# One accumulated row per token: the scatter of the experts' rows in a hybrid decoder layer

## The chip, the cores and the metric

One Trainium2 chip, of which the kernel uses 1 core. The metric is the device time of one execution in microseconds. The kernel before was run three times: 1439.99, 1440.33 and 1444.06 us, median 1440.33 us. All tensors of the interface are float32.

## What is computed

One layer over 1024 tokens of 1024 numbers: a norm with conditioning, a mixer of two branches (a convolution and an mLSTM), a residual, a second norm, a mixture of experts, a residual and a final norm. The change concerns the mixture of experts. Cut to what matters:

```
p_grp = softmax(h @ w_rg + b_rg);  g_sel = argmax(p_grp)             # one of 4 groups per token
le_sel = (h @ w_re + b_re)[token, g_sel]                              # 8 experts of that group
top_p, top_e = top_k(softmax(le_sel), 2)                              # two experts per token
w_tok = p_g * top_p / sum(top_p)
ys = (silu(xb @ w_e_gate[e]) * (xb @ w_e_up[e])) @ w_e_down[e]        # per expert, on its tokens' rows
y[token] = sum over its two experts of w_tok * ys
x = x + gate2 * y;   out = rmsnorm(x, g_final)
```

Every token thus gets two rows of 1024 numbers, from two different experts of the same group.

## The kernel before

**Order of the work.** Everything is issued in one hand-written order. The mixer comes first. Its projection is a list of jobs of 48 matrix products each (`z_cols`, L473); after the first half of a job and after its end `fill` (L290) takes one step from each of a few queues of small work: `lat` and `lat2` (the mLSTM, the convolution's norm) and `aux` (first the conditioning's remaining columns, then `clear_y`). When the jobs are over, `drain` (L299) runs what the queues still hold, and then the branches' own projections begin (`branch`, L1004; their results are named `yTrue`). At its end the mLSTM generator waits until `aux` is empty (L879), then releases buffers and gives out eight more steps (L894 to L904): each transposes one tile of 128 tokens on TensorE (`psT`, four 128x128 transposes), scales it on ScalarE (`hs`) and splits it on VectorE (`bHt`, `bLt`).

**The buffer for experts' rows.** `y_d` is a DRAM buffer of 2T = 2048 rows of 4 KB: row t for a token's first expert, row T+t for its second. `clear_y` (L448) fills it with zeros, 16 stores of 512 KB through SP's queue, with two steps of `aux` for each.

**The experts.** Their rows are worked in 25 blocks of 128 rows, in 24 units (L1460). The 16 fullest experts have a large block each (0 to 15; block 24 is a second block of expert 2's place); the other 16 share the 8 small blocks 16 to 23, two experts to a block, 64 rows each. One large and one small block alternate as large, large, small. For each block, `st_slots` (L1681) finds by a product on TensorE which token stands in which of the 128 rows (`idx`, and the row's weight `wsl`), and GpSimd gathers these tokens' rows from DRAM (`gather`, L1602, into one of three buffers `xg`). `st_x` transposes them (`tpx`), `st_gu` multiplies with the gate and up weights, `st_act` and `st_h` make the hidden rows, `st_down` (L1731) multiplies with the down weights and scales the result into `ye`. The weights come through SP's queue in pieces of 1 MB into six buffers `big`; for a large block ScalarE and VectorE split each piece into a high and a low part (`wh`, `wl`) and TensorE makes three products, for a small block the pieces go into TensorE as they are. `scatter` (L1607) then writes the rows of `ye` to `y_d`: one indirect DMA from GpSimd's queue; rows of the block that hold no token have an index out of bounds and are left out. The column of `idx` that it uses, the second, is the row of `y_d`; the first column is the token. Each such DMA waits for the one before it on `y_d`.

**The end.** The last two blocks (14 and 15, `LATE`) are not scattered: their rows stay in SBUF as `lates` and are put in token order by products with a selection matrix (`selT`, results `yl`). When the last unit begins, `load_y` (L1811) issues 16 loads of 512 KB from `y_d` through SP's queue, for eight tiles of 128 tokens two rows each. `sum_y` (L1826) adds them up: for tiles 0 and 1 straight into the residual `mg` (tile 0 on GpSimd, tile 1 on VectorE, two additions each), for the others on GpSimd into the first of the two. The final loop (L1900) makes, for each tile, the products `yl`, for tiles 4 to 7 also a product of the summed rows with the identity into the same PSUM; VectorE adds the PSUM to `mg` (and for tiles 2 and 3 the summed rows as well), ScalarE sums the squares, GpSimd makes the factor `r`, VectorE scales (`final_out`, L1894), and the tile is stored.

Of the kernel before, what the change touches and what calls it, by code (L numbers as in the profile page):

```python
# [18 lines left out]
P = 128  # L19
# [23 lines left out]
def hybrid_layer_kernel(ctx: ExitStack, tc: tile.TileContext, x, c, w_ada, b_ada, g_norm1, w_in, b_if,  # L43
# [11 lines left out]
    def tt(o, a, b, op, eng=V):  # L55
        return eng.tensor_tensor(out=o, in0=a, in1=b, op=op)  # L56

    def ts(o, a, s1, op0, s2=None, op1=None, eng=V):
        if op1 is None:
            return eng.tensor_scalar(out=o, in0=a, scalar1=s1, scalar2=None, op0=op0)  # L60
        return eng.tensor_scalar(out=o, in0=a, scalar1=s1, scalar2=s2, op0=op0, op1=op1)
# [4 lines left out]
    def mm(o, l, r, start, stop):  # L66
        return PE.matmul(o, l, r, start=start, stop=stop)  # L67
# [7 lines left out]
    mod_d = dram.tile([32, P], F32, name="mod_d")  # L75
    nM_d = dram.tile([32, P], F32, name="nM_d")
    h2_d = dram.tile([T, D], F32, name="h2_d")
    y_d = dram.tile([2 * T, D], F32, name="y_d")


    cst = ctx.enter_context(tc.tile_pool(name="cst", bufs=1, side="left"))
# [366 lines left out]
    def clear_y():  # L448
        zero = ml.tile([P, 256], F32, name="zero")
        G.memset(zero, 0.0)  # L450
        for i in range(2 * NT):
            nc.sync.dma_start(y_d[i * P:(i + 1) * P, :].rearrange("p (a n) -> p a n", n=256),
                              zero.unsqueeze(1).broadcast_to([P, 4, 256]))
            yield 0
            yield 0
# [1148 lines left out]
                             in_offset=bass.IndirectOffsetOnAxis(ap=idx[:, 0:1], axis=0),  # L1604
                             bounds_check=T - 1, oob_is_err=False)

    def scatter(src, idx):  # L1607
        G.indirect_dma_start(out=y_d[:, :], out_offset=bass.IndirectOffsetOnAxis(ap=idx[:, 1:2], axis=0),  # L1608
                             in_=src, in_offset=None, bounds_check=2 * T - 1, oob_is_err=False)

    def ovf_slots(pool, bv, name):

# [118 lines left out]
    def st_down(unit):  # L1731
        py = {b: [mps.tile([P, 512], F32, tag="m", name=f"py{b}_{hf}") for hf in range(2)] for b in unit}
        for k in range(4):
            if unit[0] in SMALL:
                if k % 2 == 0:
                    wab = [W.take() for _ in range(4)]
                for hf in range(2):
                    for n, h_ in enumerate(HALVES):
                        mm(py[unit[0]][hf][h_, :], R[unit[0]]["g"][:, k, h_],
                           wab[2 * n + k % 2][:, hf * 512:(hf + 1) * 512], k == 0, k == 3)  # L1740
                if k % 2:
                    W.used()
                continue
            wh, wl = W.take()
            for b in unit:
                gH, gL = R[b]["g"]
                for i, (a, b_) in enumerate(((gH, wh), (gL, wh), (gH, wl))):
                    for hf in range(2):
                        mm(py[b][hf], a[:, k, :], b_[:, hf * 512:(hf + 1) * 512], k == 0 and i == 0, k == 3 and i == 2)
        for b in unit:  # L1750
            d = R.pop(b)
            y = wp.tile([P, WB], F32, tag="raw", bufs=2, name=f"ye{b}")[:, 0:D]
            late = b in blocks[-LATE:]
            yhl = [wp.tile([P, WB], F32R, tag="whl", bufs=6, name=f"y{x_}{b}")[:, 0:D] for x_ in "hl"] if late else None
            for hf in range(2):
                sl = slice(hf * 512, (hf + 1) * 512)
                stt(y[:, sl], py[b][hf], d["wsl"], gt2[:, sl], OP.mult, OP.mult)
                if b == blocks[-1]:
                    split(yhl[0][:, sl], yhl[1][:, sl], y[:, sl])
            if late:  # L1760
                lates.append(yhl + [y])
            else:
                scatter(y, d["idx"])


    for r in range(FIX):
# [41 lines left out]
    def into_x1(t, a, eng=V):  # L1808
        tt(x1_of(t), x1_of(t), k3(a), OP.add, eng=eng)

    def load_y():  # L1811

        n = W.bigs_loaded
        bufs = [W.big[(n + i // 2) % len(W.big)][:, i % 2 * D:(i % 2 + 1) * D] for i in range(9)]
        bufs += [xgs[(len(blocks) + i) % 3] for i in range(3)]
        a = uo.tile([P, 2, D], F32, tag="ar", bufs=2, name="yra")
        bufs += [a[:, 0, :], a[:, 1, :]]
        bufs += [cvp.tile([P, D], F32, tag="s", bufs=4, name="yrs"), mo.tile([P, D], F32, tag="tHL", bufs=2, name="yrt")]
        gf[0] = cvp.tile([P, D], F32, tag="s", bufs=4, name="gfr")
        on_all_rows(gf[0], vec[:, 120:128])  # L1820
        for t in range(NT):
            for i in range(2):
                yin[t, i] = bufs[2 * t + i]
                nc.sync.dma_start(yin[t, i], y_d[i * T + t * P:i * T + (t + 1) * P, :])

    def sum_y(t):  # L1826
        if t < 2:
            for i in range(2):
                into_x1(t, yin[t, i], V if t else G)
        else:  # L1830
            tt(yin[t, 0], yin[t, 0], yin[t, 1], OP.add, eng=G)


    W.limit = len(W.pieces) - 2
# [52 lines left out]
    def final_norm(t, pool, o):  # L1887
        r3_ = pool.tile([P, 1], F32, tag="r3", bufs=4, name=f"r3_{t}")
        S.activation(k3(o), x1_of(t), AF.Square, scale=float(D) ** -0.5, accum_out=r3_)
        ts(r3_, r3_, RMS_EPS, OP.add, eng=G)  # L1890
        rsqrt(r3_, r3_, 1)
        return r3_

    def final_out(t, o, r3_):  # L1894
        stt(k3(o), x1_of(t), r3_, k3(gf[0]), OP.mult, OP.mult)
        (S if t == NT - 1 else nc.sync).dma_start(out[t * P:(t + 1) * P, :], o)
# [3 lines left out]
    for t in range(NT + 1):  # L1900
        if t < NT:
            if t % 2:
                ps = [mps.tile([P, 512], F32, tag="m", name=f"yl{t}_{hf}") for hf in range(2)]
            else:
                ps_ = zps.tile([P, 2, 512], F32, tag="z", name=f"yl{t}")
                ps = [ps_[:, hf, :] for hf in range(2)]
            on_pe = t >= NT - 4
            for n in range(LATE):
                for i in range(2):
                    for hf in range(2):  # L1910
                        mm(ps[hf], selT[:, n, t * P:(t + 1) * P], lates[n][i][:, hf * 512:(hf + 1) * 512],
                           n == 0 and i == 0, not on_pe and n == LATE - 1 and i == 1)
            if on_pe:
                for hf in range(2):
                    mm(ps[hf], ident, yin[t, 0][:, hf * 512:(hf + 1) * 512], False, True)
            if t + 4 < NT:
                sum_y(t + 4)
            if t % 2:
                for hf in range(2):
                    o_ = x1_of(t)[:, hf * 4:hf * 4 + 4, :]  # L1920
                    tt(o_, o_, k3(ps[hf]), OP.add)
            else:
                into_x1(t, ps_.rearrange("p a b -> p (a b)"))
            if 2 <= t and not on_pe:
                into_x1(t, yin[t, 0])
            r3[t] = final_norm(t, mo, yin[t, 1])
        if t > 0:
            final_out(t - 1, yin[t - 1, 1], r3[t - 1])

    order.__exit__(None, None, None)  # L1930

# [104 lines left out]
```

## Time and profile before

| what | value |
|---|---|
| three runs | 1439.99, 1440.33, 1444.06 us |
| the profiled execution | 1436.36 us, its span 1434.6 us |
| TensorE busy | 1304.0 us, 91% of the span |
| VectorE, ScalarE, GpSimd busy | 70%, 36%, 24% |
| mean granted clock of TensorE | 0.958 of full speed |
| DMA | 336.60 MB, mean 235 GB/s |

The profile cuts the span into 40 slices of 35.9 us and gives the busy share of each engine in each. Its rows are the place to see stages: the mixer until about 790 us, the routing until about 860 us, the experts until about 1395 us, the end.

### The profile page before, as it was taken

Reading aid. Unit: us, or ns where it says so; the run is one execution under the profiler, and the core shown is the slowest. Engines: PE = TensorE matmul, PEld = TensorE weight load, DVE = VectorE, ACT = ScalarE, POOL = GpSimd, SP = SyncE. Lnnn points to the kernel's source line nnn. Section 1 sums busy time; section 2 is a strip of 40 time slices with the busy share of each in tenths; the row PEclk is TensorE's granted clock in tenths of the full one; section 3 lists DMA queues with packets and bytes.
Section 4 is the critical chain, followed back from the end, with each engine's and each line's share of the span. In section 5 each row is a group of like instructions: output and inputs, shape, how many; then the busy total and the mean of one; then the engine's idle time right before and its main releaser. Section 6 shows DMA issues by size and latency. Waiting matters only on the chain. (4 is left out here: it accounts for less than half of the span.)

```text
span 1434.6 us, 17769 instructions
## 1 busy us (share of the span) xinstructions
PE 1304.0 (91%) x6659; PEld 981.1 (68%) x6659; DVE 1008.0 (70%) x1375; ACT 522.4 (36%) x692; POOL 337.6 (24%) x270
## 2 busy tenths in 40 slices
PE   4799888999999999999999669999999999999976
PEld 3687888879878888778888545656465655655554
DVE  6979998889966661654557786357676766764587
ACT  5233143333622225311232533225354453533442
POOL 3333455231231310124223211001011111111033
PEclk9799999999999999999999779999999999999998
DMA  9433443333454343454522449799999999999982
GB/s 287 127 118 133 140 140 118 132 118 89 132 179 131 124 135 123 162 166 159 182 70 78 187 167 377 308 379 418 413 415 396 412 399 405 414 382 415 405 332 118
DMA packets 121017, 336.60 MB, mean 235 GB/s; under 512 B 12465, under 2 KB 74205, under 8 KB 96096
## 3 DMA queue, kind: packets, MB, share of 16 engines
q1 hardware_dynamic: 106208, 291.34, 54.1%
q0 software_dynamic: 14528, 43.56, 8.1%
q8 instruction: 53, 0.87, 0.2%
q10 hardware_dynamic: 192, 0.54, 0.1%
q14 instruction: 36, 0.29, 0.1%
HBM read 302.85 MB, written 41.45 MB: 240 GB/s over the span
## 5 line engine op out<-in xcount | busy, mean ns | idle before, releaser
L56 DVE TENSOR_TENSOR wl<-big,wh 128x1024 fp32r<-128x1024 f32 x192 | 233.7, 1254 | 101.4 <-ACT wh L148 100.1
L148 ACT CAST wh<-big 128x1024 fp32r<-128x1024 f32 x192 | 193.6, 1048 | 181.6 <-DMA big<-in_w_e_gate_dram 94.4
L64 DVE SCALAR_TENSOR_TENSOR cacc<-u,vec,cacc 128x1024 f32<-128x1024 f32 x120 | 211.2, 1760 | 2.9
L67 PE MATMUL gu<-wh,tHLx 128*128 128x512 f32 x544 | 174.6, 402 | 2.8 <-ACT wh L148 1.4
L67 PE MATMUL z<-hH,wh 128*128 128x512 f32 x512 | 167.4, 409 | 7.4 <-DVE hH L377 5.1
L67 PE MATMUL z<-hL,wh 128*128 128x512 f32 x512 | 164.5, 403 | 1.2 <-DVE hL L56 1.2
L67 PE MATMUL z<-hH,wl 128*128 128x512 f32 x512 | 163.3, 400 | 0.0
L67 PE MATMUL gu<-big,tFx 128*64 128x512 f32 x512 | 122.3, 621 | 0.0
L67 PEld LDWEIGHTS gu<-wh,tHLx 128*128 128x128 f32 x544 | 99.9, 189 | 30.6 <-ACT wh L148 7.6
L67 PEld LDWEIGHTS z<-hH,wh 128*128 128x128 f32 x512 | 97.0, 193 | 29.7 <-ACT hH L380 5.1
L67 PE MATMUL gu<-wl,tHLx 128*128 128x512 f32 x272 | 109.3, 402 | 8.7 <-DVE wl L56 8.6
L67 PEld LDWEIGHTS z<-hL,wh 128*128 128x128 f32 x512 | 98.3, 192 | 25.7 <-DVE hL L56 1.9
L67 PEld LDWEIGHTS z<-hH,wl 128*128 128x128 f32 x512 | 98.1, 192 | 23.8
L1608 POOL DMA_INDIRECT y_d<-ye,idx x23 | 33.2, 1445 | 330.2 <-DVE ye L64 326.6
L56 DVE TENSOR_TENSOR wl<-raw,wh 128x1024 fp32r<-128x1024 f32 (+1 forms) x45 | 70.6, 1573 | 39.7 <-ACT wh L148 39.7
L56 POOL TENSOR_TENSOR acc<-acc,ar 128x1024 f32<-128x1024 f32 x24 | 70.8, 2951 | 62.3 <-ACT ar L572 53.4
L67 PEld LDWEIGHTS gu<-big,tFx 128*64 128x64 f32 x512 | 36.3, 142 | 69.6 <-issue 67.3
L67 PE MATMUL py<-wh,tHLh 128*128 128x512 f32 x272 | 78.4, 411 | 0.1
L67 PE MATMUL zt<-wh,hH 128*128 128x256 f32 (+1 forms) x256 | 74.9, 292 | 2.6 <-DVE u L56 1.3
L67 PE MATMUL zt<-wl,hH 128*128 128x256 f32 (+1 forms) x256 | 73.7, 288 | 2.8 <-DVE wl L56 2.8
L67 PE MATMUL zt<-wh,hL 128*128 128x256 f32 (+1 forms) x256 | 74.1, 290 | 0.0
L67 PE MATMUL o<-woH,mHL 128*128 128x512 f32 x256 | 72.8, 400 | 0.0
(404 smaller groups left out, 2209.3 us busy)
## 6 DMA issues: line engine op xcount, KB each, us to landing
big<-in_w_e_gate_dram SPq DMA_DIRECT2D x64, 1024.0 KB, 9.2
big<-in_w_e_up_dram SPq DMA_DIRECT2D x64, 1024.0 KB, 6.0
big<-in_w_e_down_dram SPq DMA_DIRECT2D x64, 1024.0 KB, 9.3
raw<-in_w_in_dram SPq DMA_DIRECT2D x38, 512.0 KB, 4.4
ar<-in_w_ada_dram SPq DMA_DIRECT2D x16, 1024.0 KB, 6.3
araw<-in_w_ada_dram SPq DMA_DIRECT2D x8, 1024.0 KB, 10.2
y_d<-zero SPq DMA_DIRECT2D x16, 512.0 KB, 5.2
big<-y_d SPq DMA_DIRECT2D x9, 512.0 KB, 9.7
```

Of the source, the lines that this page charges most:

```text
L56: return eng.tensor_tensor(out=o, in0=a, in1=b, op=op)
L64: return V.scalar_tensor_tensor(out=o, in0=a, scalar=s, in1=b, op0=op0, op1=op1)
L67: return PE.matmul(o, l, r, start=start, stop=stop)
L148: S.copy(h, src)
L1608: G.indirect_dma_start(out=y_d[:, :], out_offset=bass.IndirectOffsetOnAxis(ap=idx[:, 1:2], axis=0), in_=src, in_offset=None, bounds_check= ...
```

## The change

`y_d` has one row per token. `clear_y` clears 8 tiles in place of 16. The scatter uses the first column of `idx` (the token) and adds to the row in DRAM (`compute_op`) in place of writing it. In a small block the same token may stand twice, once in each half; such a block is therefore sent in two DMAs, each with the other half's indices pushed out of bounds by two small VectorE operations. `load_y` loads 8 tiles. `sum_y` adds tiles 0 to 3 to `mg` (even ones on GpSimd, odd ones on VectorE) and has nothing to do for the others.

```diff
-    y_d = dram.tile([2 * T, D], F32, name="y_d")
+    y_d = dram.tile([T, D], F32, name="y_d")
...
-        for i in range(2 * NT):
+        for i in range(NT):
             nc.sync.dma_start(y_d[i * P:(i + 1) * P, :].rearrange("p (a n) -> p a n", n=256),
...
-    def scatter(src, idx):
-        G.indirect_dma_start(out=y_d[:, :], out_offset=bass.IndirectOffsetOnAxis(ap=idx[:, 1:2], axis=0),
-                             in_=src, in_offset=None, bounds_check=2 * T - 1, oob_is_err=False)
+    past = rp.tile([P, 2], F32, name="past")
+    for n in range(2):
+        ts(past[:, n:n + 1], pio, 64.5, (OP.is_gt, OP.is_lt)[n], float(2 * T), OP.mult)
+
+    def scatter(b, src, idx):
+
+        rows_ = [idx[:, 0:1]]
+        if b in SMALL:
+            rows_ = []
+            for n in range(2):
+                rows_.append(mo.tile([P, 1], I32, tag=f"half{n}", bufs=2, name=f"half{n}_{b}"))
+                tt(rows_[n], idx[:, 0:1], past[:, n:n + 1], OP.add)
+        for r_ in rows_:
+            G.indirect_dma_start(out=y_d[:, :], out_offset=bass.IndirectOffsetOnAxis(ap=r_, axis=0),
+                                 in_=src, in_offset=None, bounds_check=T - 1, oob_is_err=False, compute_op=OP.add)
...
-                scatter(y, d["idx"])
+                scatter(b, y, d["idx"])
...
         for t in range(NT):
-            for i in range(2):
-                yin[t, i] = bufs[2 * t + i]
-                nc.sync.dma_start(yin[t, i], y_d[i * T + t * P:i * T + (t + 1) * P, :])
+            yin[t] = bufs[t]
+            nc.sync.dma_start(yin[t], y_d[t * P:(t + 1) * P, :])
 
     def sum_y(t):
-        if t < 2:
-            for i in range(2):
-                into_x1(t, yin[t, i], V if t else G)
-        else:
-            tt(yin[t, 0], yin[t, 0], yin[t, 1], OP.add, eng=G)
+        if t < NT - 4:
+            into_x1(t, yin[t], V if t % 2 else G)
...
-            if t + 4 < NT:
-                sum_y(t + 4)
...
-            if 2 <= t and not on_pe:
-                into_x1(t, yin[t, 0])
```

Three places show what this moves.

**TensorE, between the last job of the mixer's projection (`z5000`) and the branches' projection (`yTrue`).** Before, the seven transposed tiles psT1 to psT7 stand there in a row:

```order
L67 MATMUL z5000_4226<-hH_110,wl39_4090 128x512 x2
L897 MATMUL psT1_4293<-ident_118,WT0_2483 128x128 x4
L897 MATMUL psT2_4308<-ident_118,WT0_2483 128x128 x4
L897 MATMUL psT3_4323<-ident_118,WT0_2483 128x128 x4
L897 MATMUL psT4_4335<-ident_118,WT1_2540 128x128 x4
L897 MATMUL psT5_4347<-ident_118,WT1_2540 128x128 x4
L897 MATMUL psT6_4359<-ident_118,WT1_2540 128x128 x4
L897 MATMUL psT7_4371<-ident_118,WT1_2540 128x128 x4
L67 MATMUL yTrue_0_4408<-uH0_4217,wh40_4150 128x512 x2
```

Now three of them do:

```order
L67 MATMUL z5000_4269<-hH_110,wl39_4098 128x512 x2
L897 MATMUL psT5_4336<-ident_118,WT1_2540 128x128 x4
L897 MATMUL psT6_4351<-ident_118,WT1_2540 128x128 x4
L897 MATMUL psT7_4363<-ident_118,WT1_2540 128x128 x4
L67 MATMUL yTrue_0_4400<-uH0_4090,wh40_4181 128x512 x2
```

`aux` is empty earlier, since the clearing takes 16 steps in place of 32; psT0 to psT4 have moved up, one by one between the products of the last three jobs.

**GpSimd, around a small block (18) among the experts.** Before, each scatter is followed by a gather for a later block (`xg`):

```order
L1608 DMA y_d_92<-ye4_7608,idx4_6936 2048x1024
L1603 DMA xg2_5929<-h2_d_91,idx19_7669 128x1024
L1608 DMA y_d_92<-ye18_7774,idx18_7135 2048x1024
L1603 DMA xg0_5927<-h2_d_91,idx7_7853 128x1024
L1608 DMA y_d_92<-ye5_7979,idx5_7319 2048x1024
```

Now the small block's rows go in two DMAs, and the gather for block 7 stands behind both:

```order
L1620 DMA y_d_92<-ye4_7617,idx4_6938 1024x1024
L1603 DMA xg2_5921<-h2_d_91,idx19_7678 128x1024
L1620 DMA y_d_92<-ye18_7783,half0_18_7786 1024x1024
L1620 DMA y_d_92<-ye18_7783,half1_18_7788 1024x1024
L1603 DMA xg0_5919<-h2_d_91,idx7_7869 128x1024
L1620 DMA y_d_92<-ye5_7995,idx5_7328 1024x1024
```

The second half waits until the first has landed, and the gather waits its turn behind it.

**VectorE, in the final loop.** Before (tiles 1 to 3):

```order
L56 TENSOR_TENSOR mg_4387<-mg_4387,yl2_10563 128x8x128
L56 TENSOR_TENSOR mg_4387<-mg_4387,big0_4954 128x8x128
L64 SCALAR_TENSOR_TENSOR big1_4955<-mg_4387,r3_1_10557,gfr_10404 128x1024
L56 TENSOR_TENSOR mg_4387<-mg_4387,yl3_0_10581 128x4x128
L56 TENSOR_TENSOR mg_4387<-mg_4387,yl3_1_10582 128x4x128
L56 TENSOR_TENSOR mg_4387<-mg_4387,big2_5885 128x8x128
L64 SCALAR_TENSOR_TENSOR big0_4954<-mg_4387,r3_2_10575,gfr_10404 128x1024
```

Now:

```order
L56 TENSOR_TENSOR mg_4379<-mg_4379,yl2_10599 128x8x128
L64 SCALAR_TENSOR_TENSOR xg2_5921<-mg_4379,r3_1_10593,gfr_10452 128x1024
L56 TENSOR_TENSOR mg_4379<-mg_4379,yl3_0_10615 128x4x128
L56 TENSOR_TENSOR mg_4379<-mg_4379,yl3_1_10616 128x4x128
L64 SCALAR_TENSOR_TENSOR xg0_5919<-mg_4379,r3_2_10609,gfr_10452 128x1024
```

The additions of the summed rows for tiles 2 and 3 are gone from the loop (they stand ahead of it, one of them on GpSimd), and so are GpSimd's four additions inside the loop.

## Rows read from the trace of the kernel before

**Rows 1.** The second part of the profile's page: by 40 slices of 35.9 us the busy tenths of TensorE and of the DMA engines.
```profile
PE   4799888999999999999999669999999999999976
...
DMA  9433443333454343454522449799999999999982
```

**Rows 2.** The table of stretches: start and end, length, busy us of PE, PEld, DVE, ACT and POOL (instructions), granted TensorE clock, DMA share, GB/s.
```profile
580.00:585.00 5.00, 2.35 (x11) 1.98 (x11) 4.93 (x8) 5.00 (x18) 0.00 (x0) 0.80 0.19 79
...
860.00:1366.00 506.00, 479.90 (x2414) 291.79 (x2413) 314.92 (x357) 210.31 (x254) 56.96 (x43) 0.98 0.98 396
900.00:950.00 50.00, 49.90 (x245) 30.60 (x246) 23.71 (x27) 15.12 (x19) 4.21 (x4) 1.00 0.81 315
1040.00:1080.00 40.00, 36.89 (x192) 24.61 (x194) 30.20 (x35) 18.02 (x22) 4.99 (x4) 0.97 1.01 413
1080.00:1088.00 8.00, 8.00 (x49) 2.82 (x45) 2.82 (x3) 3.53 (x5) 0.98 (x1) 0.91 0.89 345
```

**Rows 3.** The DMA view of the experts' stretch, 860 to 1366 us: the queue of GpSimd (packets, MB, packet time as a share of 16 engines over the stretch), then GpSimd's issues with their number and the median us to landing.
```profile
q0 software_dynamic: 6192, 14.72, 7.6%
...
y_d<-ye,idx POOLq DMA_INDIRECT x23, 9.1
xg<-h_d,idx POOLq DMA_INDIRECT x20, 8.6
```

**Rows 4.** TensorE in order of time from the last products of the mixer's projection to the first of the branches': start us, us, engine, line, operation, out<-in, shapes, number, [idle before and what ended it].
```profile
571.02 0.60 PE L897 MATMUL psT<-ident,WT 128*128 128x128 f32 x4
571.37 0.70 PE L67 MATMUL z<-hH,wh 128*128 128x512 f32 x2
...
577.03 1.91 PE L897 MATMUL psT<-ident,WT 128*128 128x128 f32 x16
579.38 0.66 PE L897 MATMUL psT<-ident,WT 128*128 128x128 f32 x4 [0.45 <-ACT hs L901]
581.36 0.66 PE L897 MATMUL psT<-ident,WT 128*128 128x128 f32 x4 [1.32 <-ACT hs L901]
583.34 1.12 PE L897 MATMUL psT<-ident,WT 128*128 128x128 f32 x4 [1.32 <-ACT hs L901]
584.11 1.20 PE L67 MATMUL yTrue<-uH,wh 128*128 128x512 f32 x2
585.11 1.05 PE L67 MATMUL yTrue<-uL,wh 128*128 128x512 f32 x2
585.96 0.85 PE L67 MATMUL yTrue<-uH,wl 128*128 128x512 f32 x2
586.65 0.62 PE L67 MATMUL yTrue<-uH,wh 128*128 128x512 f32 x2
```

**Rows 5.** GpSimd and TensorE in order of time among the experts: scatters of the blocks 16, 2 and 24, then the scatter of block 18, the gather for block 7 behind it, and the transposes that read what it brought. The last line is of the view of the scatter's source line.
```profile
912.49 1.74 POOL L1608 DMA_INDIRECT y_d<-ye,idx  x1 [16.29 <-DVE ye L64]
...
944.95 1.01 POOL L1608 DMA_INDIRECT y_d<-ye,idx  x1 [16.92 <-DVE ye L64]
949.55 1.24 POOL L1608 DMA_INDIRECT y_d<-ye,idx  x1 [3.59 <-DMA y_d<-ye,idx]
...
1039.26 1.71 POOL L1608 DMA_INDIRECT y_d<-ye,idx  x1 [15.42 <-DVE ye L64]
1045.17 1.26 POOL L1603 DMA_INDIRECT xg<-h_d,idx  x1 [4.19 <-PE tph L1647]
...
1062.57 1.03 POOL L1603 DMA_INDIRECT xg<-h_d,idx  x1 [2.78 <-issue]
...
1068.35 1.15 PE L1647 MATMUL tpx<-ident,xg 128*128 128x128 f32 x8
...
DMA to landing us min/median/max: 3.8/9.1/11.2
```

**Rows 6.** VectorE's price for a two-column operation on integers, from the groups of the experts' stretch (number | busy us, mean ns | idle before).
```profile
L60 DVE TENSOR_SCALAR idx<-sv 128x2 int32<-128x2 f32 x20 | 3.4, 170 | 0.7
```

**Rows 7.** The end in order of time, GpSimd's and SP's queues: the last scatter (block 23), the last weight loads, the first loads from `y_d`.
```profile
1356.43 1.70 POOL L1608 DMA_INDIRECT y_d<-ye,idx  x1 [26.99 <-DVE ye L64]
1359.59 3.20 SPq L204 DMA_DIRECT2D big<-in_w_e_down_dram  x2
1365.79 9.73 SPq L1824 DMA_DIRECT2D big<-y_d  x9
```

**Rows 8.** The end in order of time, VectorE and TensorE: the additions ahead of the loop, the last split, TensorE's wait for it; in the loop the two additions of summed rows and the last tiles.
```profile
1384.96 6.72 DVE L56 TENSOR_TENSOR mg<-mg,big 128x1024 f32<-128x1024 f32 x2
1391.61 2.35 DVE L56 TENSOR_TENSOR wl<-big,wh 128x1024 fp32r<-128x1024 f32 x2
1392.88 0.73 PE L67 MATMUL py<-wl,tHLh 128*128 128x512 f32 x2 [1.80 <-DVE wl L56]
...
1408.01 2.98 DVE L56 TENSOR_TENSOR mg<-mg,big 128x1024 f32<-128x1024 f32 x1
...
1413.41 3.21 DVE L56 TENSOR_TENSOR mg<-mg,big 128x1024 f32<-128x1024 f32 x1
...
1418.84 1.88 PE L67 MATMUL yl<-yrs,ident 128*128 128x512 f32 x4
...
1424.79 1.27 DVE L56 TENSOR_TENSOR mg<-mg,yl 128x512 f32<-128x512 f32 x2
...
1428.29 1.28 DVE L64 SCALAR_TENSOR_TENSOR yrt<-mg,r,gfr 128x1024 f32<-128x1024 f32 x1 [1.03 <-POOLq L1936]
```

More of the change, by code (lines that the diff above doesn't have):

```diff
@@ L1813, in load_y @@
         n = W.bigs_loaded
[L1814 to L1818, printed above, removed]
+        bufs = [xgs[(len(blocks) + i) % 3] for i in range(3)]
+        bufs += [W.big[(n + i // 2) % len(W.big)][:, i % 2 * D:(i % 2 + 1) * D] for i in range(5)]
         gf[0] = cvp.tile([P, D], F32, tag="s", bufs=4, name="gfr")
@@ L1914, in hybrid_layer_kernel @@
                 for hf in range(2):
-                    mm(ps[hf], ident, yin[t, 0][:, hf * 512:(hf + 1) * 512], False, True)
-            if t + 4 < NT:
-                sum_y(t + 4)
+                    mm(ps[hf], ident, yin[t][:, hf * 512:(hf + 1) * 512], False, True)
             if t % 2:
@@ L1923, in hybrid_layer_kernel @@
                 into_x1(t, ps_.rearrange("p a b -> p (a b)"))
-            if 2 <= t and not on_pe:
-                into_x1(t, yin[t, 0])
-            r3[t] = final_norm(t, mo, yin[t, 1])
+            r3[t] = final_norm(t, mo, yin[t])
         if t > 0:
-            final_out(t - 1, yin[t - 1, 1], r3[t - 1])
+            final_out(t - 1, yin[t - 1], r3[t - 1])
     order.__exit__(None, None, None)
```

## The prediction

> **What bounds the kernel now.** I read the profile from the slices down to the waits. The slices come first [rows 1]: TensorE is busy nearly throughout the mixer, and the DMA engines idle more than half of that time; from about 860 us on the DMA row stands at 9, and so it stays until the end of the experts. The table of stretches sharpens that [rows 2]: from 860 to 1366 us the DMA share is 0.98 and TensorE is busy 479.9 of 506 us. Weights flow at some 400 GB/s and TensorE has 5% to spare, so both are near their limits there, and DMA is the one that is full. What the scatter costs lies in this stretch: GpSimd's queue, that is 23 scatters and 20 gathers, takes 7.6% of the sixteen engines' time for 14.72 MB [rows 3]. The end, from 1366 us, is a chain of VectorE, TensorE and waits [rows 7, 8]. And the order of TensorE's instructions says that a place in the mixer, which no line of the diff names, is touched as well [rows 4].
>
> All sums are made against the profiled execution, 1436.36 us; the median of the three runs, 1440.33, is 3.97 us above it. Two versions of this kernel that differ by less than 0.3%, some 4.3 us, can hardly be told apart.
>
> **The mixer: 5.4 us less.** With half the stores to clear, the queue of small work is empty earlier, and four of the seven transposed tiles leave the gap between the two projections. Before, that gap lasts from 577.03 to 584.11, 7.08 us: seven groups at 0.48 us (1.91 us for four) and 3.1 us of waits for ScalarE, which copies each tile out (0.45, 1.32, 1.32) [rows 4]. Afterwards three groups are left, 1.43 us, and the four that moved up cost 0.35 us each between other products (571.02 to 571.37), 1.40 us: a gain of 4.25. The buffers that the last three need were freed long before, so ScalarE holds nothing up. The granted clock was 0.80 in the stretch from 580 to 585 us [rows 2], after TensorE had stood idle, and the first three pairs of products after the gap start 1.00, 0.85 and 0.69 us apart, 2.54 in all, where three pairs at full clock take 1.38 (0.46 each, as in the projection before): another 1.16. Sum 5.4; at least 3 if one wait stays. TensorE is busy on to the experts, so the gain reaches the end. The eight stores themselves lie where DMA is less than half full, and cost nothing now.
>
> **The end: 5.9 us less.** Before, VectorE's two additions for tile 1 take 6.72 us, 3.4 each, since GpSimd adds beside it; an operation of the same size at the very end, with GpSimd idle, takes 1.28 [rows 8]. They stand ahead of the last split `wl`, for which TensorE waits 1.80 us. Afterwards there are again two additions (tiles 1 and 3), but GpSimd has two additions in all in place of eight, and they are over by then; the wait goes, if the rows are there in time. In the loop VectorE loses the additions of 2.98 and 3.21 us. Before, TensorE had ended tile 7's products at 1420.7, and VectorE took them up at 1424.79, 4.1 us late; then the chain to 1428.29 is fixed. Without the additions VectorE has 14 operations of some 1.25 us ahead of tile 7, 17.5 us from about 1398, and waits for TensorE. So 1.8 + 4.1 = 5.9.
>
> Are the rows in time? The last scatter goes out at 1356.43 and the loads wait until 1365.79 [rows 7]. Now block 23 goes in two halves, one after the other's landing: 9.1 us (the median) twice and 1.7 between puts the loads at some 1376.5, 11 us later. But the weights are then in (last issue by 1363 [rows 7], landing some 9 us later, as GpSimd's do under the same load [rows 3]), and half as many loads share empty queues: at the 413 GB/s of the full stretch a load of 512 KB takes 1.3 us, the fourth lands at about 1383, and VectorE needs the second and fourth from 1385 on [rows 8]. At 11.2 us each, the longest landing seen [rows 5], 4 us of the gain would be lost; that is the bound.
>
> **The small operations: 1.4 us more.** Sixteen of them on VectorE; the nearest row is a two-column operation at 0.17 us [rows 6]. That is 2.7 us, between `ye` and the next split. VectorE has spare time (315 of 506 us busy [rows 2]), but its waits are for short chains: half is counted, with 0 and 2.7 as ends.
>
> **The scatter: 12.5 us more.** The scatters move as many new rows as before, since a half leaves out the other's. What an accumulating row costs no row of this trace shows. Their present share: 7.6% of 506 us is 38.5 us for 43 DMAs of like rows, so 23 of 43, 20.6 us of all sixteen engines [rows 3]. The lower end is 0: the row is read, added to and written in the time that the write takes now. The upper one is as much again: the old row is as many bytes as the new one, and fetching it is what the gathers do at the same rate. I take the doubling, since those bytes must come through the same engines, but not all of it lies on the path. From 900 to 950 us the DMA share is only 0.81 [rows 2], 9.5 us free, which covers the three scatters there [rows 5], 2.7 us. From 1080 to 1088 it is 0.89, 0.9 us free; six such periods of a small and two large blocks, those of the blocks 17 to 22, lie behind it, another 5.4. So 20.6 - 2.7 - 5.4 = 12.5, between 0 and 20.6. The Trainium skill, "Collectives: The Full Stack", section "The bandwidth ceiling: the fold count and why AG ≠ RS ≠ AR", speaks against this change: an addition inside a DMA engine needs two source reads on one ring, and the rate fell there from 62.28 to 32.35 GB/s, by 1.93. By that rule, estimated, the 20.6 us would grow by 19.2 in place of 20.6; no run here shows it yet.
>
> **The new wait on GpSimd.** In seven small blocks the second half waits for the first, and behind it stands the gather for a later block, on which TensorE's transposes wait. From the scatter of block 18 at 1039.26 to the transposes that read that gather at 1068.35 there are 29.1 us [rows 5]. They now hold the landing L of the first half, the second's issue and the gap behind it (1.7 and 2.8), the gather's issue and landing (1.3 and 8.6): L + 14.4. With L = 9.1, 5.6 us are left, and up to L = 14.7 nothing is late. The eight added issues fall where GpSimd idles.
>
> **Sum.** -5.4 - 5.9 + 1.4 + 12.5 = +2.6: 1439.0 against the profiled execution, 1442.9 on the scale of the median. Forecast: no change that can be told, two gains given back to the DMA engines.
>
> **The rivals.** *The addition is nearly free.* A row then holds its engine no longer than a write does, and the extra is 0: 2.6 - 12.5 = -9.9, 1430.4. For it: the rate in the full stretch goes up and down (413 and 345 GB/s in neighbouring stretches [rows 2]), so the engines may have more to give than the share tells, and a read and a write use two directions. Against it: the share stands at 1.01 and the old rows have to come from somewhere. It decides as long as the extra is under 5.6 us. *The addition holds its engine much longer*, slower than before: fetch, add and write one after another, three times the present time. 41.2 us, less the 8.1 that are free, make 33.1 for 12.5: 1463.5. Its place is the full stretch; it decides once the extra passes 14.2 us. For it: nothing in the trace bounds an operation that it doesn't hold. Against it: a landing under load is mostly waiting behind weights (3.8 us at the least, 9.1 in the median [rows 5]), so the rows' own time is the smaller part. *The two halves make the gathers late.* Once L passes 14.7 us, each of seven small blocks stalls TensorE by the excess: at L = 18, 7 x 3.3 = 23 us, 1466. Against it: the longest landing is 11.2.
>
> **How the numbers follow.** The doubling has 0.43; its own range, with an extra of 9 to 20.6 us, is 1439.4 to 1451.0, of which 0.29 lies within 0.3% (up to 14.2 us of extra) and 0.14 above. The nearly free addition has 0.36, all of it faster. The much longer one has 0.15, the late gathers 0.06, both slower. So faster 0.36, same 0.29, slower 0.35. The range runs from 1427 (the free addition, with 3 us more at the end than counted) to 1460, which leaves out the upper part of the two slow cases.
>
> **What would show it.** In the profile of the changed kernel: three groups of psT between the projections, the first product of `yTrue` some 5 us earlier against the last of `z`, and the granted clock of the stretch behind it at 1; the share of GpSimd's queue from 860 to 1366 at about twice 7.6%, and the last weight load some 8 us later than 1359.59 (12.5 + 1.4 less 5.4); landings of the scatters up to 14 us and no wait of TensorE or of ScalarE for a gather; loads from `y_d` some 11 us behind the last first half, no wait of VectorE for them; tile 7's addition right behind its products. If the queue's share stays at 7.6% the free addition is right; at 20% or more, the long one. The forecast is wrong at its core if the experts' stretch keeps its length, or grows by more than 20 us.

## The result

The changed kernel takes 1452.31 us (median of 7 runs, 1448.12 to 1454.66), the kernel before 1440.33 in the same series (7 runs, 1438.76 to 1445.50): a ratio of 1.0074, 95% interval 1.0056 to 1.0092. (The ratio is estimated from all runs; the medians alone, 12.0 us apart, would give 1.0083.) So it is slower, by some 0.7% and clear of noise. The range held it; the forecast, 1442.9, was 9.4 us too low. The profiled execution of the changed kernel took 1454.66 us, its span 1452.5.

### The profile after

The table of stretches of the changed kernel (columns as in [rows 2]):

```profile
580.00:585.00 5.00, 5.00 (x30) 4.25 (x29) 1.56 (x3) 3.69 (x10) 0.53 (x1) 1.00 0.25 104
860.00:1380.00 520.00, 477.72 (x2374) 287.69 (x2373) 307.21 (x365) 202.70 (x246) 98.92 (x50) 0.98 0.98 378
900.00:950.00 50.00, 49.91 (x244) 31.79 (x244) 20.28 (x26) 12.85 (x17) 6.59 (x4) 1.00 0.84 314
```

The experts' stretch is as full of DMA as before (0.98), but it moves 378 GB/s in place of 396, and lasts longer. Its DMA view, 860 to 1380 us, answers to [rows 3]; below it the page's line on memory traffic:

```profile
q0 software_dynamic: 7056, 14.60, 11.5%
...
xg<-h_d,idx POOLq DMA_INDIRECT x20, 10.6
y_d<-ye,idx POOLq DMA_INDIRECT x15, 10.5
y_d<-ye,half POOLq DMA_INDIRECT x15, 11.3
...
HBM read 298.66 MB, written 41.45 MB: 234 GB/s over the span
```

Now 14.60 MB hold the engines for 11.5% of 520 us, 59.8 us, where 14.72 MB held them for 38.5. (Block 23's two halves have not landed in this window; the block has 0.13 MB.) GpSimd's queue around block 18, in order of time, answers to [rows 5]:

```profile
1046.02 5.79 POOL L1620 DMA_INDIRECT y_d<-ye,half  x1 [14.90 <-DVE half L56]
1061.25 2.36 POOL L1620 DMA_INDIRECT y_d<-ye,half  x1 [9.45 <-DVE wl L56]
1063.92 1.06 POOL L1603 DMA_INDIRECT xg<-h_d,idx  x1 [0.31 <-issue]
1073.32 1.58 POOL L1620 DMA_INDIRECT y_d<-ye,idx  x1 [8.34 <-DVE tHLh L56]
```

The second half goes out 15.2 us after the first (the releaser that is named, a `wl` of VectorE, has nothing to do with it; the second half waits for the first one's landing), and the gather stands behind it, as the order of instructions said.

In the mixer, the rows that answer to [rows 4], with ScalarE's activation (`g`) of an earlier job ahead and the first product behind the branches (`x1p`) after them. First of before:

```profile
404.32 1.03 ACT L980 ACTIVATE g<-z 128x1024 f32<-128x1024 f32 x1
...
693.38 1.03 PE L1141 MATMUL x1p<-ident,mg 128*128 128x128 f32 x8
```

then of the changed kernel:

```profile
406.52 1.03 ACT L980 ACTIVATE g<-z 128x1024 f32<-128x1024 f32 x1
...
581.06 1.47 PE L897 MATMUL psT<-ident,WT 128*128 128x128 f32 x12
582.29 0.70 PE L67 MATMUL yTrue<-uH,wh 128*128 128x512 f32 x2
582.83 0.62 PE L67 MATMUL yTrue<-uL,wh 128*128 128x512 f32 x2
583.29 0.63 PE L67 MATMUL yTrue<-uH,wl 128*128 128x512 f32 x2
...
690.81 1.03 PE L1141 MATMUL x1p<-ident,mg 128*128 128x128 f32 x8
```

The gap is 1.23 us where it was 7.08, and the pairs behind it start 0.46 to 0.54 us apart. At the end, the rows that answer to [rows 7] and [rows 8]:

```profile
862.96 2.35 POOL L1620 DMA_INDIRECT y_d<-ye,idx  x1 [11.33 <-DVE ye L64]
...
1379.74 2.36 POOL L1620 DMA_INDIRECT y_d<-ye,half  x1 [26.22 <-DVE half L56]
1382.96 3.20 SPq L204 DMA_DIRECT2D big<-in_w_e_down_dram  x2
1390.21 5.57 POOL L1620 DMA_INDIRECT y_d<-ye,half  x1 [8.12 <-DVE wl L56]
1398.88 1.28 SPq L1832 DMA_DIRECT2D xg<-y_d  x3
1408.98 1.21 DVE L56 TENSOR_TENSOR mg<-mg,xg 128x1024 f32<-128x1024 f32 x1
1410.12 1.21 DVE L56 TENSOR_TENSOR mg<-mg,big 128x1024 f32<-128x1024 f32 x1
1412.18 2.36 DVE L56 TENSOR_TENSOR wl<-big,wh 128x1024 fp32r<-128x1024 f32 x2 [0.85 <-ACT wh L148]
1441.86 1.88 PE L67 MATMUL yl<-big,ident 128*128 128x512 f32 x4
1442.91 0.69 DVE L56 TENSOR_TENSOR mg<-mg,yl 128x512 f32<-128x512 f32 x1 [0.28 <-PE yl L67]
1446.69 1.28 DVE L64 SCALAR_TENSOR_TENSOR big<-mg,r,gfr 128x1024 f32<-128x1024 f32 x1 [1.03 <-POOLq L1937]
```

VectorE's additions take 1.21 each, and tile 7's is taken up as TensorE makes it. From these rows the stages can be set against the prediction. Each is the difference to the profile of before; the last column is a second profile of the unaltered changed kernel (e9, below).

| stage | predicted | change | repeat |
|---|---|---|---|
| start to the activation at 404 us | 0 | +2.2 | +3.3 |
| on to `x1p` (mixer) | -5.4 | -4.8 | -5.0 |
| on to the first scatter (routing) | 0 | +3.1 | +1.3 |
| on to block 23's scatter (experts) | +13.9 | +22.8 | +22.3 |
| on to the last scaling (end) | -5.9 | -4.9 | -6.4 |
| the last four | +2.6 | +16.2 | +12.3 |

The first row is no part of the change: over 14 profiled executions of all kernels here, whose programs are alike up to there, ScalarE's first activation of a mixer's job came between 80.8 and 84.9 us, and the two profiles of before are among the earliest (81.1 and 80.8). It is one reason why the profiles differ by 15 to 18 us and the medians by 12; another is that the first of them was the slowest of the seven runs of the change.

### The profile page after: what moved, and what is told of

The parts are those of the page before. It is cut to its first block, busy times and chain, and to the rows that moved or that the text cites. A ratio compares the mean times of both kernels' runs of the same rounds, so it can differ in the third digit from the quotient of the medians.

```text
span 1452.5 us, 17758 instructions
## 1 busy us (share of the span) xinstructions
PE 1310.4 (90%) x6659; PEld 984.7 (68%) x6659; DVE 998.9 (69%) x1391; ACT 522.2 (36%) x692; POOL 370.2 (25%) x272
## 3 DMA queue, kind: packets, MB, share of 16 engines
HBM read 298.66 MB, written 41.45 MB: 234 GB/s over the span
## 5 line engine op out<-in xcount | busy, mean ns | idle before, releaser
L67 PE MATMUL gu<-wh,tHLx 128*128 128x512 f32 x544 | 180.6, 414 | 8.1 <-ACT wh L148 6.1
L67 PEld LDWEIGHTS gu<-wh,tHLx 128*128 128x128 f32 x544 | 103.6, 196 | 37.1 <-ACT wh L148 13.4
L67 PE MATMUL gu<-wl,tHLx 128*128 128x512 f32 x272 | 112.7, 414 | 9.2 <-DVE wl L56 9.2
L1620 POOL DMA_INDIRECT y_d<-ye,half x16 | 56.8, 3550 | 206.4 <-DVE half L56 133.5
L67 PEld LDWEIGHTS gu<-big,tFx 128*64 128x64 f32 x512 | 35.7, 136 | 78.2 <-issue 59.8
L67 PE MATMUL zt<-wl,hH 128*128 128x256 f32 (+1 forms) x256 | 73.8, 288 | 2.9 <-DVE wl L56 2.9
L67 PEld LDWEIGHTS gu<-wl,tHLx 128*128 128x128 f32 x272 | 53.4, 196 | 30.6 <-DVE wl L56 19.2
```

## The experiments

Theory A: an accumulated row holds the DMA engines for twice as long, and all of that lies on the path. Theory B: the two halves of a small block, one behind the other's landing, hold back gathers and issues. Each ratio is to the kernel before, run beside it on the same chip; "stretch" is the time from the first scatter to block 23's, "end" from there to the end of the last scaling.

| run | us | ratio (95%) | stretch | end |
|---|---|---|---|---|
| before | 1440.33 | 1 | 494.0 | 73.1 |
| the change | 1452.31 | 1.0074 (1.0056 to 1.0092) | 516.8 | 68.2 |
| e1 halves, no addition | 1426.68 | 0.9909 (0.9890 to 0.9929) | 495.3 | 64.6 |
| e2 addition, whole blocks | 1449.61 | 1.0079 (1.0058 to 1.0100) | 514.5 | 63.8 |
| e3 neither | 1426.38 | 0.9918 (0.9899 to 0.9938) | 493.5 | 63.7 |
| e4 before, 16 steps | 1436.03 | 0.9972 (0.9959 to 0.9984) | 494.8 | 73.8 |
| e5 before, clearing apart | 1440.18 | 1.0019 (1.0004 to 1.0035) | 493.1 | 73.3 |
| e6 rows written twice | 1446.20 | 1.0056 (1.0040 to 1.0071) | 515.5 | 64.9 |
| e7 addition at the end | 1442.00 | 1.0025 (1.0011 to 1.0039) | 495.9 | 74.4 |
| e8 change, 32 steps | 1450.90 | 1.0091 (1.0064 to 1.0118) | 516.5 | 68.1 |
| e9 change again | 1449.31 | 1.0081 (1.0056 to 1.0106) | 516.3 | 66.8 |
| e10 before again, one run | 1436.46 | - | 494.4 | 73.0 |
| e11 sums on TensorE | 1437.86 | 1.0005 (0.9987 to 1.0022) | 493.0 | 76.2 |
| e12 tile 1 on TensorE | 1437.25 | 0.9978 (0.9965 to 0.9992) | 493.4 | 73.8 |

### The addition or the halves: e1, e2, e3

e1 takes the addition away and keeps the halves:

```diff
-                                 ..., bounds_check=T - 1, oob_is_err=False, compute_op=OP.add)
+                                 ..., bounds_check=T - 1, oob_is_err=False)
```

> The changed kernel with a plain write in place of the accumulating one; the small blocks still go in two halves. What it computes differs: a token's second row overwrites its first. Theory A (an accumulated row holds the DMA engines for twice a written row's time, and all of it lies on the path): the experts' stretch falls back from 517 us (first scatter to that of block 23) to 494 to 498, GpSimd's queue from 11.5% to some 7.7%, time 1430 to 1434. Theory B (the halves: the second waits for the first's landing and holds back gathers, issues and end): the stretch stays at 513 to 517, time 1447 to 1453. A mixture would lie between, and its place is the share of each.

e2 keeps the addition and takes the halves away (it clears all 16 tiles, in the change's 16 steps); e3 is e2 without `compute_op`. The cut edit of e2:

```diff
-        rows_ = [idx[:, 0:1]]
-        if b in SMALL:
...
+        rows_ = [idx[:, 1:2]]
...
-        for i in range(NT):
+        for i in range(2 * NT):
...
             yield 0
-            yield 0
```

> The changed kernel with the accumulating scatter, but each block in one DMA: it adds to the row of the first or the second expert (2048 rows, all cleared, in the same 16 steps of the queue of small work). The second rows are left out of the sum, the loads at the end are the same eight. Theory A: the stretch stays at 514 to 517 us, GpSimd's queue at 11 to 11.5%, time 1448 to 1452 (the half's second wait at the end, some 5 us, may be gained or be covered). Theory B: the stretch falls to 494 to 498, time 1428 to 1434.

> The same with a plain write: neither halves nor an addition, but the mixer's order and the end of the changed kernel. The second experts' rows are left out of the sum. Both theories: the stretch is that of before, 494 us, GpSimd's queue 7.6%. It measures the two gains alone: if the prediction's terms hold (5.4 in the mixer, 5.9 at the end) 1429; if the mixer's gain is lost in the routing stage, as the one profile of the changed kernel makes it look, some 1434.

The four kernels (with the change itself) make a table of two by two: the addition costs 23 us (e2 against e3, ratios 0.016 apart) and 24 with halves (the change against e1), the halves nothing that the times show. The traces show a little: with halves the stretch and the end are some 3 us longer without the addition (e1 against e3) and 5 to 7 with it (e9 and the change against e2), but e2 and e3 clear twice as much in the same steps, and their mixer, from the activation near 408 us to `x1p`, is 2.2 to 2.5 us longer, which hides part of that. The times of e1 and e3 lie under what was expected, since the end gained more than had been counted. The queue's row and the first, seventh and last scatter, first of e3:

```profile
q0 software_dynamic: 6192, 14.72, 7.6%
...
863.20 1.74 POOL L1614 DMA_INDIRECT y_d<-ye,idx  x1 [11.34 <-DVE ye L64]
990.56 1.72 POOL L1614 DMA_INDIRECT y_d<-ye,idx  x1 [11.65 <-DVE ye L64]
1356.74 1.70 POOL L1614 DMA_INDIRECT y_d<-ye,idx  x1 [27.14 <-DVE ye L64]
```

then of e2 (the queue rows are of 860 to 1366 us and 860 to 1392 us, so that all 23 scatters lie in both):

```profile
q0 software_dynamic: 6192, 14.73, 11.6%
...
864.83 2.35 POOL L1614 DMA_INDIRECT y_d<-ye,idx  x1 [11.33 <-DVE ye L64]
994.54 2.30 POOL L1614 DMA_INDIRECT y_d<-ye,idx  x1 [11.63 <-DVE ye L64]
1379.32 2.29 POOL L1614 DMA_INDIRECT y_d<-ye,idx  x1 [27.61 <-DVE ye L64]
```

Engine time (the share times the window, in us of all sixteen engines) rises from 38.5 to 61.7 us, by 23.2 or 1.0 for each scatter, and the stretch by 21.0. Up to the seventh scatter e2 has lost 2.4 us, so some of the extra is hidden there; over the 16 scatters behind it 18.6, that is 1.16 each, and nothing is hidden. Theory A holds but for that first part. One thing goes along with it that no run takes apart: between the first scatter and block 23's TensorE's granted clock is 0.97 in e2 and 0.99 in e3 (0.98 in the change, 1.00 in e1), and of the 21.0 us TensorE is idle for 5.3 and busy for 15.7, with the same number of products. That the DMA share stays at 0.98 while the rate falls from 396 to 380 GB/s is why the engines are taken for the bound. In e1 the queue's row (860 to 1366 us) is that of before:

```profile
q0 software_dynamic: 7200, 14.67, 7.7%
...
861.58 1.74 POOL L1620 DMA_INDIRECT y_d<-ye,idx  x1 [11.34 <-DVE ye L64]
971.47 5.20 POOL L1620 DMA_INDIRECT y_d<-ye,half  x1 [16.60 <-DVE half L56]
1366.48 5.86 POOL L1620 DMA_INDIRECT y_d<-ye,half  x1 [7.81 <-DVE wl L56]
```

Theory B falls: with the same waits between halves the stretch is 495.3, 1.8 more than e3's, and 516.8 against 514.5 with the addition. The changed kernel's trace shows why: in its stretch TensorE's products never wait for a gather, and its weight loads do so four times, for 3.5 us in all.

### An addition, or just twice the traffic: e6

Against e3 each block's rows are written a second time, to a buffer `y2_d` that nobody reads:

```diff
+            G.indirect_dma_start(out=y2_d[:, :], out_offset=..., in_=src, ...)
```

> The kernel of e3 (plain writes, whole blocks, second experts' rows left out of the sum), but each block's rows are written twice, the second time to another buffer that nobody reads. No addition anywhere: it doubles the scatter's bytes and nothing else. If an accumulated row costs what twice its bytes cost: the experts' stretch 513 to 516 us, GpSimd's queue 11.5 to 12%, time 1446 to 1450, as e2. If the addition itself is slow (fetch, add and write one after another) and bytes alone are cheaper: stretch 498 to 508, time 1431 to 1441. If two writes cost more than an addition, over 1452.

Its queue's row (860 to 1393 us, all 46 scatters), first scatter and block 23's:

```profile
q0 software_dynamic: 9504, 22.61, 10.9%
...
864.70 1.74 POOL L1615 DMA_INDIRECT y_d<-ye,idx  x1 [11.13 <-DVE ye L64]
1380.21 1.70 POOL L1615 DMA_INDIRECT y_d<-ye,idx  x1 [28.11 <-DVE ye L64]
```

Another 7.9 MB of plain rows cost 19.6 us of engine time (58.1 less 38.5) and 22.0 us of the stretch, about what the addition costs. So some 19.6 us is what the scatter of these rows itself takes, and an accumulating one 42.8 (23.2 more), 2.2 times as much. The addition costs about what a second pass of the same rows through full engines costs; that the engines really make such a pass, to fetch the old rows, is argued from this price and not shown. Neither the queue's packets and bytes nor the page's memory line show it: e3, too, reads 298.66 MB and writes 41.45. That line is no measure of what moved: for e6 it has 12.06 MB more written, 23 whole blocks of 128 rows, where the queue moved 7.9.

### The mixer's part: e4, e5, e8, with e9 and e10

e4 and e8 change the number of steps alone (`before`, one `yield` per store in place of two; the change, four in place of two); e5 clears the second half of the rows elsewhere:

```diff
-        for i in range(2 * NT):
+        for i in range(NT):
...
     for g_ in xgs:
         S.activation(k3(g_), ..., AF.Copy, scale=0.0)
+    for i in range(NT):
+        nc.sync.dma_start(y_d[T + i * P:T + (i + 1) * P, :], xgs[0])
```

> The kernel before with one step of the queue of small work per cleared tile in place of two, so that the 16 stores take as many steps as the eight of the change; nothing else. It is the mixer's part alone. The gap between the projections falls from 7.1 us to some 1.3. If that reaches the end (prediction): 1435, 0.37% less than before. If the routing stage takes it back: 1440, no difference.

> The kernel before, where the queue of small work clears the rows of the first expert alone (eight stores in 16 steps, as in the change), and the other eight stores go out in the routing stage, from a buffer that holds zeros there. Nothing else. It is the mixer's part of the change without the denser stores of e4. The prediction's term (5.4 us, all of it reaching the end): 1434 to 1435. If e4 was held back by its 16 stores in half the steps: some 7 less than before, 1432 to 1433. If the routing stage takes the gain back: 1438 to 1440.

> The changed kernel with four steps of the queue of small work per cleared tile in place of two, so that the eight stores take 32 steps, as the sixteen of before did. The transposed tiles go back into the gap between the projections; scatter and end stay those of the change. If the mixer's term of the prediction reaches the end: 5.4 us more than the changed kernel (1457 to 1458, 1.2% over before). If it gets lost on the way: the changed kernel's time, 1452 (0.7% over).

> The changed kernel once more, unaltered, beside e8 on the same chip: 0.7 to 0.8% over before. Its second trace shows how far the stages of one program differ from one execution to the next: the time from the first scatter to that of block 23 and the end should repeat to 1 us (516.8 and 68.2); the time to the first scatter may differ by some us.

> The kernel before once more, unaltered, for a second trace. The profiled execution of before was 4 us under the median. If that lies ahead of the experts, the first scatter comes at some 866 us in place of 862.4, with the stretch (494.0) and the end (73.1) repeated to 1 us; else one of these two is longer.

e8 puts the gap back into the change: from the activation near 407 us to `x1p` it takes 287.6 us, e9 284.1, so 3.5 are gained there. But from `x1p` to the first scatter e8 takes 168.4 and e9 170.4: 2.0 are lost again, and the medians differ by 1.6, inside the intervals. Where they go, TensorE's transposes of the second gathered block show, in before:

```profile
837.98 1.94 PE L1661 MATMUL tpx<-ident,xg 128*128 128x128 f32 x8 [4.48 <-DMA xg<-h_d,idx]
```

and in e9:

```profile
838.00 1.94 PE L1673 MATMUL tpx<-ident,xg 128*128 128x128 f32 x8 [5.28 <-DMA xg<-h_d,idx]
```

e9 is 1.7 us earlier than before at `x1p`, and at these transposes it stands at the same time: TensorE comes sooner and waits longer for a gather.

e5 came out otherwise than expected. Its mixer is 5.0 us shorter up to `x1p`, yet its first scatter comes 2.1 us later than before's. The eight stores go out from 793.42 on, right behind the store of `h2_d`, from which the gathers read; GpSimd issues the first gather at 808.06 after 15.1 us of idleness (before: 802.17 after 5.7), and TensorE waits for it, which it does not in before:

```profile
812.99 1.94 PE L1649 MATMUL tpx<-ident,xg 128*128 128x128 f32 x8 [6.90 <-DMA xg<-h_d,fidx]
```

From 793 to 805 us the DMA share is 1.00 and more, where before has 0.81 up to 800 us and 0.11 after it. That the stores delay the gather by filling the engines is argued from this order; no run takes it apart.

e4's median is 0.28% under before. Its own trace doesn't show a gain (the time from the activation near 408 us to the last scaling is 1025.8, before 1025.3). Of the two kernels with the same mixer (below), e12 is 0.22% under before; e11 has no gain, but its end is 3.1 us longer. How much of a shorter mixer the medians keep stays open. In e10 the expected late start did not come; the second profile of before repeats the first to 0.4 us at every stage.

### Another end: e7, e11, e12

Three kernels with the whole result and plain writes. e7 lets DMAs add the second rows to the first in SBUF after the weights; e11 and e12 (on e4's mixer) let GpSimd add the rows and TensorE take the sum in, for all tiles and for tile 1.

```diff
# e7 (cut), against the change
+        for t in range(NT):
+            G.dma_start(yin[t], y_d[T + t * P:T + (t + 1) * P, :], accum_op=OP.add)
# e11 (cut), against before; e12: on_pe = t >= NT - 4 or t == 1
-            on_pe = t >= NT - 4
+            on_pe = True
```

> A whole result again: two rows per token, plain writes, whole blocks, the clearing as in e5; at the end the eight loads of the first rows as in the change, and then eight loads of the second rows on GpSimd's queue that add to the first in SBUF. The additions inside the DMA engines are thus moved behind the weights, where the queues are empty. If they cost twice their 4 MB, some 20 us from 1376, tile 0 is there at about 1384 and tile 7 at about 1402, before the loop needs it: e3's end (63.7 us from block 23's scatter to the last scaling, 73.1 before) and e5's mixer, together 1424 to 1428. If VectorE's first additions wait for them: 1430 to 1436.

> The kernel before with the 16-step clearing of e4, and another end: for all eight tiles GpSimd adds the two rows and TensorE adds the sum into the products' PSUM by the identity, so VectorE has none of the rows' additions (before: four operations). Rows are written plainly, as before. If VectorE's additions were the end's price: wait for the last split gone (1.8), last tile some 2 us sooner, since TensorE gets four times 0.94 us more to do; with e4's 3.6 this makes 1431 to 1434. If GpSimd's eight sums (2.7 each from 1378 on) come too late for TensorE: end as before, 1435 to 1438.

> The kernel of e4 (before, with the clearing in 16 steps), where tile 1 alone goes the way of tiles 4 to 7: GpSimd adds its two rows, TensorE adds the sum into the products by the identity, and VectorE's two additions ahead of the last split, 6.7 us beside GpSimd, are gone. The whole result, plain writes. If these two additions set the end's start: the wait of TensorE for the last split (1.8 us) goes and the end falls from 73.1 to some 70 to 71; with e4's 0.28% the time is 1432 to 1434, 0.4 to 0.5% under before. If GpSimd's sums, 2.7 us later each, hold the loop instead, as in e11: the end stays at 73 to 76 and the time at e4's or above.

None shortens the end. e7 is slower than either of its expectations. In it (its mixer and routing are e5's) the rows come late; VectorE's additions:

```profile
1390.64 1.23 DVE L56 TENSOR_TENSOR mg<-mg,xg 128x1024 f32<-128x1024 f32 x1 [5.00 <-DMA xg<-y_d]
1396.54 4.36 DVE L56 TENSOR_TENSOR mg<-mg,big 128x1024 f32<-128x1024 f32 x1 [4.67 <-DMA big<-y_d]
```

It waits 9.7 us. In e11 TensorE is the bound of the loop (3.6 us per tile), in e12 the last split starts only 1.6 us sooner behind block 23's scatter than in before (33.6 us for 35.2), and VectorE then waits 3.4 us for the products of tiles 0 and 1: the end is e4's. So no version here beats both kernels by a gain that a trace explains; e4 and e12, 0.2 to 0.3% under before, are the fastest whole ones.

## Why the prediction was right or wrong

The forecast was no change that can be told. The kernel is slower, by more than the 0.3% that the prediction had set as the limit (it had given slower 0.35 and the same 0.29); the time lies in the upper half of the range. By the prediction's own sign it is wrong at its core: the experts' stretch grew by 22.8 us (22.3 in e9), more than the 20 that it names, where the sum has 13.9.

**The mixer, 5.4 less: right as far as it went.** Up to `x1p` 4.8 and 5.0 were gained, with the granted clock at 1.00 behind the gap. That "the gain reaches the end" the traces do not bear out: TensorE is busy on to the routing, but there it waits for transfers, and 1.3 to 3.1 us went into them. e4's median leaves open how much.

**The end, 5.9 less: right in sum (4.9 and 6.4), not in its parts.** With whole blocks the gain is 9.4 (73.1 to 63.7, e3), more than the 1.8 and 4.1 that were counted; the halves with an addition take 3 to 4.5 of it back (66.8 and 68.2 against 63.8 in e2). The loads go out 19.1 us behind the first half, before 9.4 behind the scatter: 9.8 later, 11 were counted. VectorE does not wait for them, as was said; the price is another. GpSimd's two additions come later with them, and now run beside VectorE's work on `sel`, the selection matrix, for which TensorE waits. In the changed kernel:

```profile
1402.27 2.35 POOL L56 TENSOR_TENSOR mg<-mg,xg 128x1024 f32<-128x1024 f32 x1 [6.49 <-DMA xg<-y_d]
1405.63 3.43 DVE L56 TENSOR_TENSOR sel<-sel 128x1024 bf16<-128x1024 bf16 x2
1405.87 2.63 POOL L56 TENSOR_TENSOR mg<-mg,xg 128x1024 f32<-128x1024 f32 x1 [1.25 <-DMA xg<-y_d]
```

in e2:

```profile
1397.82 5.31 POOL L56 TENSOR_TENSOR mg<-mg,xg 128x1024 f32<-128x1024 f32 x2 [16.21 <-DMA xg<-y_d]
1404.13 1.28 DVE L56 TENSOR_TENSOR sel<-sel 128x1024 bf16<-128x1024 bf16 x2
```

Beside GpSimd the two take 3.43 us (in before, too), alone 1.28. The prediction counted this slowing for tile 1's additions alone: with whole blocks these 2 us are gained as well, with halves they are lost again.

**The scatter, 12.5 more: this step failed.** The doubling was right: 20.6 us of present engine time were taken from the queue's share, e6 makes it 19.6, and 23.2 were added (e2). The Trainium skill's rule ("Collectives: The Full Stack", "The bandwidth ceiling: the fold count and why AG ≠ RS ≠ AR"), that an addition needs two source reads, gave 19.2 more; the price agrees within 4 us (2.2 times for its 1.93), though the two reads appear in no count of bytes or packets here. What failed is the discount of 8.1 us taken as free, and of it the 5.4. That came from one window of 8 us with a share of 0.89 [rows 2]. Whole periods of before have none of it:

```profile
1039.00:1107.00 68.00, 64.03 (x327) 39.03 (x325) 45.71 (x52) 30.51 (x37) 8.08 (x7) 0.97 1.00 407
1107.00:1174.00 67.00, 62.90 (x323) 38.45 (x322) 44.62 (x51) 29.50 (x36) 7.87 (x6) 0.97 0.99 404
```

The dip of one window was made up for in the next. From 900 to 950 the share is really lower, and some 3.6 us were hidden in e2 up to the seventh scatter (2.4 lost, where six times 1.0 were added); the 2.7 had this right. Without the discount of the periods the sum would have been 1448.3, with none 1451.0, the upper end of the doubling's own range; the median is 1452.31. Two of the signs did not follow from the sum either: with the scatters alone doubled the queue's share comes to 11.7%, not to twice 7.6%, and with three times their time to 15.7%, not 20. The measured 11.5 and 11.6% (the change and e2) fit the doubling.

**The small operations, 1.4 more: not shown by themselves.** They take 0.15 us each, and all that the halves add in the stretch is 1.8 and 2.3 (e1 against e3, the change against e2). **The new wait on GpSimd: right, but by luck.** Of all scatters the landings have a median of 10.8 us and a maximum of 14.6, under the 14.7 that were allowed, and gathers hold TensorE's weight loads for 3.5 us. But L, the first half's landing, was put at 9.1: in five of the seven small blocks of the stretch the second half goes out 15.0 to 15.3 us behind the first (block 18's rows above are one of them), so the first landed after more than 14, and the margin was 0.1 us.

Of the rivals, the free addition is excluded by e2 and e3, the late gathers by e1, and the long one by the share, 11.5% where three times the time would make 15.7.

## What to carry to other kernels

An accumulating scatter cost here about what writing its rows twice costs (23.2 and 19.6 us of engine time more); where DMA is the bound, price it as bytes of that stretch and count all of it, unless a whole period shows engines idle. Whether a stretch has DMA time to spare is read from whole periods of the work, not from a short window, whose dip the next one may fill. A gain ahead of a wait for a transfer is worth only what the transfer lets through.

## What the runs showed beside that

- An indirect DMA with at least half of its 128 rows out of bounds occupied GpSimd for up to 5.8 us, with an addition (5.79 at 1046.02) and without (5.20 and 5.86 in e1); a whole block takes 1.0 to 1.7, and with an addition 1.6 to 2.4 (e2). The other half of the same block takes 2.36 (at 1061.25); what makes the difference is open.
- Denser stores cost the mixer something: with 16 stores in 16 steps the job after the activation near 408 us takes 20.9 us (e4), with 16 in 32 steps 18.4 (before), with eight in 16 steps 18.5 (e9), with eight in 32 steps 16.9 (e8).
